# A two-layer trunk on one core: stored head outputs turned among the last projections, the last head's second half behind half 0, adds inside an MLP product, and four residual tiles in other buffers

## The chip, the cores and the metric

The kernel runs on one core of a Trainium2 chip. The metric is the device time of one execution in microseconds (us), as the median of the timed runs. The engines are TensorE (PE; its weight loads are PEld), VectorE (DVE), ScalarE (ACT), GpSimd (POOL) and SyncE (SP), whose queue issues nearly all the transfers (DMA). Each engine works through its own instructions in order; semaphores join them.

## The reference, cut to what matters

One sequence of 1024 tokens with 1024 features passes two layers in fp32. Layer 0 mixes with a gated MLP and a gated delta rule, layer 1 with differential attention over 8 heads. Each layer then has a squared-ReLU MLP and a gated per-layer embedding.

```python
def reference(x, p, ...):
    h = x
    for layer in range(DEPTH):                      # DEPTH = 2
        if layer % 2 == 0:
            ...
            h = h + jnp.concatenate([a_out, b_out], axis=-1) @ w_out_e[i]
        else:
            hn = rms_norm(h, ln_mix_o[i])
            o = diff_attention(hn @ w_qkv_o[i], attn_q_gain[i], attn_k_gain[i], diff_lambda[i],
                               attn_sub_gain[i], lam_init)
            h = h + o @ w_out_o[i]
        hn = rms_norm(h, ln_mlp[layer])
        h = h + jnp.square(jax.nn.relu(hn @ w_mlp1[layer])) @ w_mlp2[layer]
        gate = jax.nn.sigmoid(rms_norm(h, ln_ple[layer]) @ w_ple_gate[layer])
        h = h + (p[layer] @ w_ple_proj[layer]) * gate
    return h
```

## The kernel before, in words

**Layout.** Activations lie with features on the partitions: 8 tiles of 128 features (index m), each split into two halves of 512 tokens (index h, "half 0" and "half 1"). Every fp32 operand is split into a rounded part `hi` and a remainder `lo` (ScalarE casts, VectorE subtracts), and `mm3` makes three matmuls of each product. Large products use Strassen-like schemes: seven products of half-size operands with sums before and after them.

**Order.** A scheduler that simulates the engines decides the order of instructions within the data dependences and pool buffers; the order in which the code is written only breaks ties. `pe.floor` and `behind` add an order without a wait. Generators interleave streams that are independent.

**Stages in time.** Layer 0's mixing runs to about 490 us, its MLP to about 1130, its embedding to 1210; attention from 1210 to about 1720; `mix_out` (the output projection) to 1764; the second MLP to 2400; `ple_out`, the last stage, to the end.

**Attention (`attention`).** `pump` is called 264 times. Each call pulls units of the q, k and v projections as `MARKS` demands (168 units in all; a mark (i, u) says that u units are done by call i), and after call `TAIL` also steps `tails`. Of each head's output, `o` is scaled on GpSimd (line 1099) and stored in `o_dram`. `put_halves` loads the stored outputs of heads 0 to 5 through a ring of four tiles (`ol`), and `put_o` turns each with four transposes into a `tr` tile of PSUM, from which `ohi` (ScalarE) and `olo` (VectorE) are made. `mix_part` multiplies these heads with their part of the output weights and writes the sum to `h_dram`. Head 7 is the last; its outputs are turned directly by two closures in `close`. `ss` (line 938) and `qk` are tiles of a head's score path.

**`mix_out(h, ...)`.** It adds the remaining heads (`KA` = (6, 5): from head 6 in half 0, from head 5 in half 1) for each m: it loads `a` from `h_dram`, multiplies, adds (line 1257), squares into the sum `sqs` (lines 240, 241) and stores. After half 0, `rms(0, ...)` sums `sqs` over partitions with `ones` (tile `aux`), takes the mean `ms` (256), the power on GpSimd (258), broadcasts the row factors into `rb` with four matmuls and a copy (265), and scales the eight tiles into `hi` and `lo` (1268, 1272, 1273) for the MLP. In half 1 the same follows at the start of the MLP. For layer 0 `late` lets the first two output tiles begin with the operands that are there first.

**MLP.** `product2(n)` is one of the seven products of the second matrix (in the order 1, 6, 5, 3, 7, 4, 2). Its loop over 16 kt makes the left operand (`left`, adds on line 282), loads and splits the right one (`g`), and multiplies. `u` holds sums shared between the products, which are added into `acc`.

**`ple_out`.** Also seven products. Weight halves come through a ring of eight raw tiles (`raw`, line 653) and are combined by VectorE (643). `by_token` holds the activations written back token by token (522), from which residual rows are read (703). The norm of half 1 (`ones`, `ms`) is taken in the middle of the first product.

Of the kernel before, what the change touches and what calls it, by code (L numbers as in the profile page):

```python
# [18 lines left out]
P = 128  # L19
# [13 lines left out]
MARKS = ((64, 50), (192, 144), (223, 168))  # L33
TAIL = 220
# [80 lines left out]
class Trunk:  # L115
# [132 lines left out]
    def rms(self, half, sqs, ms=None, rows=True):  # L248
# [10 lines left out]
        rb = None  # L259
        if rows:  # L260
            pb = self.aux_ps()
            for t in range(4):
                self.pe.matmul(pb[:, t * P : (t + 1) * P], lhsT=r[:, t : t + 1].to_broadcast([P, P]), rhs=self.ident, start=True, stop=True)
            rb = self.sp.tile([P, HT], F32, tag=f"rb{half}", name=self.nm("rb"), bufs=1)
            nc.scalar.copy(rb, pb)
        return r, rb

    def mlp(self, x, x_tags, gain, w1, w2, gain_next, h_dram, p, last):
# [358 lines left out]
    def ple_out(self, pT, acc, by_token, gain, wg, wpj, out):  # L634
# [115 lines left out]
        rows(0, 0, [self.raw(1, HT)[:, 0] for _ in R])  # L750
# [142 lines left out]
    def attention(self, w_qkv, w_out, gain_next, h_dram):  # L893
# [219 lines left out]
        def put_halves():  # L1113
# [42 lines left out]
        def tails():  # L1156
            puts = put_halves()
            for hf in range(2):
# [70 lines left out]
    def mix_out(self, h, acc, w_out, h_dram, gain_next, k0=0, late=0):  # L1229
# [6 lines left out]
        for m in range(KT):  # L1236
# [6 lines left out]
            if late and m == 0:  # L1243
                begun.append(self.mm_ps())
                for q, k in itertools.product(range(2), range(late, n)):
                    self.mm3((ps, begun[0])[q], w.at(k, slice(q * P, (q + 1) * P)), self.mixed[h][k0 + k], k == late, False)
                    yield
            for i in range(n - late if late and m < 2 else 0, n):
                k = (i + late) % n
# [4 lines left out]
                self.pe.floor = None  # L1254
                if i < n - 1:
                    yield
# [5 lines left out]
        if h == 0:  # L1262
            self.rb[0] = self.rms(0, self.sqs[0])[1]
            self.rb_mark = self.pe.mark
            lows = []
            for m in range(KT):
                a = acc(m)
                inst = nc.vector.scalar_tensor_tensor(a, a, gain_next[:, m : m + 1], self.rb[0], ALU.mult, ALU.mult)
                if m > 1:
                    self.pe.behind(inst, lows[m - 2])  # L1270
                hi, lo = self.hs_new[0][m] = self.hs_parts(0, m)
                nc.scalar.copy(hi, a)  # L1272
                lows.append(nc.vector.tensor_tensor(lo, a, f32(hi), ALU.subtract).ins.name)  # L1273
# [7 lines left out]
    def even_mix(self, first, rows_of_rest, rest_of_x, w_in, ws, bs, conv, a_log, dt_bias, v_gain, o_gain, masks, w_out, gain_next, h_dram):  # L1281
# [539 lines left out]
        def mixing():  # L1821
# [10 lines left out]
            yield from beside(self.mix_out(0, acc, w_out, h_dram, gain_next, late=G), side, 4, 8)  # L1832
# [110 lines left out]
def trunk(tc, x, p, ln_mix_e, w_in_e, gmlp_v_gain, gmlp_ws, gmlp_bs, gdn_conv, gdn_a_log, gdn_dt_bias, gdn_out_gain,  # L1943
          w_out_e, ln_mix_o, w_qkv_o, attn_q_gain, attn_k_gain, diff_lambda, attn_sub_gain, w_out_o, ln_mlp, w_mlp1,
          w_mlp2, ln_ple, w_ple_gate, w_ple_proj, masks, out):
    with ExitStack() as ctx:
# [54 lines left out]
        for layer in range(2):  # L2001
# [15 lines left out]
            for _ in T.mix_out(1, lambda m: acc_of(m, 1), (w_out_e, w_out_o)[layer][0], h_dram, gain[3 * layer + 1], KA[1] * layer):  # L2017
# [52 lines left out]
```

## Time and profile before

| quantity | value |
|---|---|
| median of 3 runs | 2499.21 us (2496.64 to 2500.72) |
| profiled execution | 2507.63 us, its span 2505.9 us |
| mean granted TensorE clock | 0.997 |
| PE busy | 2472.7 us, 99% of the span, 13567 matmuls |
| DVE, ACT, POOL busy | 1866.3, 1289.0, 301.9 us |
| chain that ended last | PE 89%, DMA 4%, DVE 4% |
| DMA read, written | 322.95 MB, 136.33 MB |

A row of waits names the engine, the tile that it works on, the engine and tile that it waited for with the line in the kernel, and then the total, the number of times and the longest. A row of a timeline gives the start, the duration, the engine, the line, the operation, out<-in with the shape, and in brackets the idle time before it with its releaser. Busy times of PE include the pipelined end of a matmul.

### The profile page before, as it was taken

The numbers are of one execution on the slowest core, as the hardware profiler recorded it, in microseconds if no ns is written. First come the engines' busy times: TensorE is split into PE (matmuls) and PEld (weight loads), VectorE is DVE, ScalarE is ACT, GpSimd is POOL, SyncE is SP. The second block draws the span as 40 slices with busy tenths as digits, with TensorE's granted clock in tenths as the row PEclk, the third lists the DMA queues.
The fourth block names the chain that finished last, engine by engine and source line by source line (L and its number), as shares of the span: only waits on it lengthen the run. The fifth ranks groups of instructions, "written<-read, shape, count | busy, mean of one in ns | idle before, by whom it ended". The sixth has DMA issues, their size and how long they took to land.

```text
span 2505.9 us, 39836 instructions
## 1 busy us (share of the span) xinstructions
PE 2472.7 (99%) x13567; PEld 2109.4 (84%) x13567; DVE 1866.3 (74%) x3643; ACT 1289.0 (51%) x2584; POOL 301.9 (12%) x272
## 2 busy tenths in 40 slices
PE   9999999999999999999999999999999999999999
PEld 7898897888888877888899999987788888888877
DVE  7777876688667879566568888885886677788678
ACT  6543443465455434454456766664654455445443
POOL 0211230000000000000234443431000000000000
PEclk9999999999999999999999999999999999999999
DMA  8384645457556856553347776799375558657873
GB/s 251 115 246 110 169 144 172 142 163 237 175 190 214 264 173 201 183 175 118 115 99 168 162 170 157 168 244 285 127 231 194 178 186 282 214 186 204 234 218 110
DMA packets 567924, 461.96 MB, mean 184 GB/s; under 512 B 256676, under 2 KB 429736, under 8 KB 567720
## 3 DMA queue, kind: packets, MB, share of 16 engines
q1 hardware_dynamic: 533912, 455.21, 60.3%
q10 hardware_dynamic: 33808, 4.20, 1.1%
q8 instruction: 107, 1.75, 0.3%
q14 instruction: 97, 0.79, 0.1%
HBM read 322.95 MB, written 136.33 MB: 183 GB/s over the span
## 4 chain that ended last, share of the span: by engine, by line
PE 89%; DMA 4%; DVE 4%; issue 1%; SPq 1%; ACT 1%; POOL 0%; ACTq 0%; DVEq 0%; POOLq 0%
PE mm L76 78%; PE po L76 3%; PE qk L76 3%; PE aux L76 2%; DMA raw<-in_w_ple_gate_dram 1%; PE tr L79 1%; DMA raw<-in_w_mlp_dram 0%; DVE w L222 0%; DMA spill<-early 0%; DMA guv<-uv_dram 0%; PE pvn L76 0%; PE aux L79 0%; PE pkq L76 0%; PE pks L76 0%; PE py L76 0%
## 5 line engine op out<-in xcount | busy, mean ns | idle before, releaser
L76 PE MATMUL mm<-g,w 128*128 128x512 f32 x2592 | 603.6, 395 | 2.3 <-DVE acc L282 1.8
L221 ACT CAST w<-raw 128x512 fp32r<-128x512 f32 x598 | 364.9, 616 | 445.7 <-PE mm L76 355.5
L76 PEld LDWEIGHTS mm<-g,w 128*128 128x128 f32 x2592 | 486.8, 188 | 116.7 <-ACT g L221 2.2
L76 PE MATMUL mm<-hi,w 128*128 128x512 f32 x1728 | 554.9, 397 | 0.3 <-ACT hi L1272 0.3
L76 PE MATMUL mm<-w,hi 128*128 128x256 f32 (+2 forms) x2528 | 505.7, 295 | 3.0 <-ACT t L1499 2.5
L222 DVE TENSOR_TENSOR w<-raw,w 128x512 fp32r<-128x512 f32 (+1 forms) x510 | 349.0, 691 | 172.8 <-ACT w L221 162.5
L76 PEld LDWEIGHTS mm<-w,hi 128*128 128x128 f32 x2528 | 403.4, 189 | 18.2 <-ACT t L1499 2.7
L76 PEld LDWEIGHTS mm<-hi,w 128*128 128x128 f32 x1728 | 324.9, 189 | 73.8 <-ACT hi L1272 0.7
L76 PE MATMUL mm<-w,lo 128*128 128x256 f32 (+2 forms) x1264 | 369.1, 293 | 0.8 <-DVE lo L222 0.8
L76 PE MATMUL mm<-lo,w 128*128 128x512 f32 x864 | 341.3, 395 | 0.9 <-DVE lo L1273 0.9
L76 PE MATMUL mm<-t,w 128*128 128x512 f32 x1152 | 270.7, 394 | 1.2 <-ACT w L221 1.2
L76 PEld LDWEIGHTS mm<-t,w 128*128 128x128 f32 x1152 | 216.6, 188 | 52.1 <-ACT w L221 1.6
L76 PEld LDWEIGHTS mm<-w,lo 128*128 128x128 f32 x1264 | 238.8, 189 | 6.8 <-DVE lo L222 1.2
L76 PEld LDWEIGHTS mm<-lo,w 128*128 128x128 f32 x864 | 163.2, 189 | 37.8 <-DVE lo L1273 1.4
L222 DVE TENSOR_TENSOR g<-graw,g 128x512 fp32r<-128x512 f32 x216 | 147.5, 687 | 10.4 <-DMA gd<-g 7.2
L221 ACT CAST g<-graw 128x512 fp32r<-128x512 f32 x216 | 132.7, 617 | 40.3 <-DMA graw<-gd 15.1
L1048 ACT ACTIVATE lg<-lg,nm 128x128 f32<-128x128 f32 (+7 forms) x128 | 99.2, 776 | 79.0 <-DVE nm L1045 78.1
L258 POOL TENSOR_TENSOR r<-ms,mhalf 128x4 f32<-128x4 f32 x12 | 12.9, 1072 | 1003.6 <-DVE ms L256 978.0
L222 POOL TENSOR_TENSOR w<-raw,w 128x512 fp32r<-128x512 f32 (+1 forms) x88 | 115.5, 1332 | 142.6 <-ACT w L221 93.5
L348 ACT ACTIVATE g<-g 128x512 f32<-128x512 f32 x96 | 60.5, 631 | 117.9 <-DVE g L282 114.1
L1045 DVE CUSTOM_DVE_ANT_0 lg<-qk,al 128x512 f32<-128x512 f32 (+3 forms) x128 | 74.7, 587 | 25.8 <-PE qk L76 19.9
L76 PE MATMUL mm<-ohi,w 128*128 128x512 f32 x256 | 86.8, 405 | 0.5 <-DVE t L1225 0.5
(331 smaller groups left out, 3523.0 us busy)
## 6 DMA issues: line engine op xcount, KB each, us to landing
raw<-in_w_mlp_dram SPq DMA_DIRECT2D x352, 256.0 KB, 3.5
graw<-gd SPq DMA_DIRECT2D x224, 256.0 KB, 3.0
gd<-g SPq DMA_DIRECT2D x192, 256.0 KB, 3.1
raw<-in_w_ple_gate_dram SPq DMA_DIRECT2D x76, 256.0 KB, 3.6
acc<-h_dram SPq DMA_DIRECT2D x64, 256.0 KB, 4.4
keep<-in_w_mlp_dram SPq DMA_DIRECT2D x64, 256.0 KB, 4.5
raw<-in_w_in_e_dram SPq DMA_DIRECT2D x60, 256.0 KB, 3.8
h_dram<-acc SPq DMA_DIRECT2D x48, 256.0 KB, 2.7
```

The costliest lines, as they stand in the source:

```text
L76: self._next(self.engine.matmul(*a, **k))
L79: self._next(self.engine.transpose(*a, **k))
L221: self.nc.scalar.copy(hi, src)
L222: (lo_engine or self.nc.vector).tensor_tensor(lo, src, f32(hi), ALU.subtract)
L258: nc.gpsimd.tensor_tensor(r, ms, self.mhalf[:, 0:4], ALU.pow)
L348: nc.scalar.activation(g, src, AF.Relu)
L1045: nc.vector.tensor_tensor_reduce(out=lg[:, k0:k1], in0=ps[:, : k1 - k0], in1=al[:, u0 + k0 : u0 + k1], scale=-1.0, scalar=3.0e38 if c == 0 ...
L1048: nc.scalar.activation(lg[:, :n], lg[:, :n], AF.Exp, bias=nm[:, r, nch - 1 : nch], scale=-1.0, accum_out=me.sums[:, b, r : r + 1])
```

## The change

1. `MARKS` and `TAIL` are other numbers, and `put_halves` pauses after its first four loads. So those loads and the six turns of half 0 start as soon as 160 units are done, among the last projections, which now reach up to call 227.
2. In `mix_out` of layer 1, head 7's second half is turned after all of half 0 rather than in its middle, and the first two tiles of half 1 begin with heads 5 and 6. The sum of squares of half 0 stays behind half 0; the broadcast of the row factors and the scaling are deferred (`self.later`) to tile m = 4 of half 1.
3. In the fifth product of both layers' MLP, eight adds of `u` get places at kt 6 to 13; four stay behind the product.
4. In `ple_out`, the four residual rows (0, 0, q) are loaded into tiles of another pool (`lo1q`), no longer into the raw ring.

```diff
-MARKS = ((64, 50), (192, 144), (223, 168))
-TAIL = 220
+MARKS = ((64, 50), (192, 144), (227, 168))
+TAIL = 205
...
-        rb = None
-        if rows:
-            pb = self.aux_ps()
...
-        return r, rb
+        return r, self.rows(half, r) if rows else None
+
+    def rows(self, half, r):
+        pb = self.aux_ps()
...
-        def product2(n, ps=None, beside={}):
+        def product2(n, ps=None, beside={}, adds={}):
...
+                if kt in adds:
+                    q, m, h = adds[kt]
+                    tt(acc[m][h], acc[m][h], u[q], ALU.add)
...
-        ps = product2(5, beside={4: (0, 4), 8: (0, 0), 12: (1, 4)})
+        ps = product2(5, beside={4: (0, 4), 8: (0, 0), 12: (1, 4)}, adds={**{6 + q: (q, 4 + q, 0) for q in range(4)}, **{10 + q: (q, q, 0) for q in range(4)}})
...
-            for m, h in ((q, 0), (4 + q, 0), (4 + q, 1)):
-                tt(acc[m][h], acc[m][h], u[q], ALU.add)
+            tt(acc[4 + q][1], acc[4 + q][1], u[q], ALU.add)
...
-        rows(0, 0, [self.raw(1, HT)[:, 0] for _ in R])
+        rows(0, 0, [self.hp.tile([P, HT], F32, tag=f"lo1{q}", name=self.nm("rows")) for q in R])
...
             for n in range(4):
                 load(n)
+            yield
...
             puts = put_halves()
+            next(puts)
...
-                if h == 1 and k0 and (m, i) == (6, 0):
-
-                    self.pe.floor = self.rb_mark
+                if h == 1 and k0 and (m, i) == (4, 0):
+                    self.pe.floor = self.pe.mark
+                    self.later()
+                    self.pe.floor = None
...
-            self.rb[0] = self.rms(0, self.sqs[0])[1]
-            self.rb_mark = self.pe.mark
+            self.r[0] = self.rms(0, self.sqs[0], rows=False)[0]
+
+            def rows():
+                self.rb[0] = self.rows(0, self.r[0])
...
+            self.later = rows
+            if not k0:
+                self.later()
...
-                    if n + 1 in (4 * (KT - KA[0]), 6 * (KT - KA[0])):
+                    if n + 1 in (4 * (KT - KA[0]), 8 * (KT - KA[0])):
                         close.pop(0)()
-            for _ in T.mix_out(1, ..., KA[1] * layer):
+            for _ in T.mix_out(1, ..., KA[1] * layer, first=(0, 1) if layer else ()):
```

Three places in the order. The first is PE at the start of the last head: `tr<-ol` is a turn of a stored output, `mm<-ohi,w` the output projection, `po<-v,aT` a value product. Before:

```order
L79 MATMUL tr_18080<-ident,ol_18021 128x128 x2
L76 MATMUL po_18091<-v_16712,aT_17934 128x128 x4
L76 MATMUL po_18091<-v_16712,aT_17936 128x128
L76 MATMUL mm_18197<-ohi_18031,w_18179 128x512
L76 MATMUL mm_18197<-olo_18032,w_18179 128x512
L76 MATMUL mm_18197<-ohi_18031,w_18180 128x512
L76 MATMUL mm_18197<-ohi_18066,w_18179 128x512
L79 MATMUL tr_18100<-ident,ol_18021 128x128 x4
```

Now, where `mm<-w,lo` and `mm<-w,hi` of 256 columns are projections:

```order
L76 MATMUL mm_18051<-w_17394,lo_12434 128x256
L76 MATMUL mm_18051<-w_17394,hi_12437 128x256
L79 MATMUL tr_17952<-ident,ol_17676 128x128 x4
L76 MATMUL mm_18051<-w_17395,hi_12437 128x256
L76 MATMUL qk_18035<-ks_17269,qh_17822 128x512
L76 MATMUL qk_18035<-ks_17269,ql_12490 128x512
```

The turns of half 0 moved from among the output projection to among the projections of the last heads.

The second is PE in `mix_out`, around the turn of head 7's second half (`tr<-ident,o`). Before, the products behind it (`mm_19224`) are still of half 0:

```order
L76 MATMUL mm_19372<-olo_19078,w_19313 128x512
L76 MATMUL mm_19372<-ohi_19077,w_19314 128x512
L79 MATMUL tr_19214<-ident,o_18776 128x128 x4
L76 MATMUL mm_19224<-ohi_19068,w_19177 128x512
L76 MATMUL mm_19224<-olo_19069,w_19177 128x512
L76 MATMUL mm_19224<-ohi_19068,w_19178 128x512
```

Now half 0 ends twelve rows above this piece, and `mm_19325` and `mm_19278` are of half 1:

```order
L76 MATMUL mm_19325<-olo_19078,w_19266 128x512
L76 MATMUL mm_19325<-ohi_19077,w_19267 128x512
L76 MATMUL aux_19249<-ones,sqs_19112 128x1 x4
L79 MATMUL tr_19240<-ident,o_18785 128x128 x4
L76 MATMUL mm_19278<-ohi_18781,w_19260 128x512
L76 MATMUL mm_19278<-olo_18782,w_19260 128x512
```

The turn moved behind half 0 and its sum of squares, which stands directly in front of it.

The third is DVE in `ple_out`, from the last square of half 1 (`sqs`) to the mean `ms`; `raw<-raw,raw` is a difference of two weight halves, `w<-raw,w` a remainder. Before:

```order
L241 TENSOR_TENSOR sqs_24915<-sqs_24915,t_25400 128x512
L222 TENSOR_TENSOR w_25594<-raw_25590,w_25593 128x512
L222 TENSOR_TENSOR w_25601<-raw_25597,w_25600 128x512
L643 TENSOR_TENSOR raw_25828<-raw_25828,raw_25830 128x512
L222 TENSOR_TENSOR w_25834<-raw_25828,w_25833 128x512
L643 TENSOR_TENSOR raw_25837<-raw_25837,raw_25839 128x512
L256 TENSOR_SCALAR ms_25533<-aux_25528 128x4
```

Now:

```order
L241 TENSOR_TENSOR sqs_24915<-sqs_24915,t_25400 128x512
L222 TENSOR_TENSOR w_25594<-raw_25590,w_25593 128x512
L639 TENSOR_TENSOR raw_25837<-raw_25837,raw_25839 128x512
L222 TENSOR_TENSOR w_25601<-raw_25597,w_25600 128x512
L222 TENSOR_TENSOR w_25834<-raw_25828,w_25833 128x512
L639 TENSOR_TENSOR raw_25846<-raw_25846,raw_25848 128x512
L222 TENSOR_TENSOR w_25843<-raw_25837,w_25842 128x512
L639 TENSOR_TENSOR raw_25855<-raw_25855,raw_25857 128x512
L256 TENSOR_SCALAR ms_25533<-aux_25528 128x4
```

The first difference moved in front of the last square, and two further ones in front of `ms`. On SP the weight loads moved up to where the row loads stood, and the row loads into the MLP's seventh product.

More of the change, by code (lines that the diff above doesn't have):

```diff
@@ L258, in rms @@
         nc.gpsimd.tensor_tensor(r, ms, self.mhalf[:, 0:4], ALU.pow)
-        rb = None
-        if rows:
-            pb = self.aux_ps()
[L262 to L265, printed above, removed]
-        return r, rb
+        return r, self.rows(half, r) if rows else None
+    def rows(self, half, r):
+        pb = self.aux_ps()
+        for t in range(4):
+            self.pe.matmul(pb[:, t * P : (t + 1) * P], lhsT=r[:, t : t + 1].to_broadcast([P, P]), rhs=self.ident, start=True, stop=True)
+        rb = self.sp.tile([P, HT], F32, tag=f"rb{half}", name=self.nm("rb"), bufs=1)
+        self.nc.scalar.copy(rb, pb)
+        return rb
     def mlp(self, x, x_tags, gain, w1, w2, gain_next, h_dram, p, last):
@@ L1226, in mix_part, with mix_out @@
             nc.sync.dma_start(h_dram[m, :, cols], res)
-    def mix_out(self, h, acc, w_out, h_dram, gain_next, k0=0, late=0):
+    def mix_out(self, h, acc, w_out, h_dram, gain_next, k0=0, first=()):
         nc = self.nc
@@ L1831, in mixing @@
             side = second_gates()
-            yield from beside(self.mix_out(0, acc, w_out, h_dram, gain_next, late=G), side, 4, 8)
+            yield from beside(self.mix_out(0, acc, w_out, h_dram, gain_next, first=range(G, KT)), side, 4, 8)
             for _ in side:
```

32 lines of the change are left out of this document (16 added, 16 removed).

## The prediction

> **What bounds the kernel now.** I read the page's busy lines first.
>
> ```profile
> span 2505.9 us, 39836 instructions
> PE 2472.7 (99%) x13567; PEld 2109.4 (84%) x13567; DVE 1866.3 (74%) x3643; ACT 1289.0 (51%) x2584; POOL 301.9 (12%) x272
> ```
>
> TensorE works for 2472.7 of 2505.9 us, so 33.2 us are idle in all. The change takes no matmul away. Hence the whole stake is a part of those 33.2 us, plus time lost at a lower clock. Next came the PE's waits over the whole span, then those of 1600 to 1820 us, of 2400 to 2450 and of 930 to 955. The columns are the total, the times and the longest.
>
> ```profile
> PE aux L76 <- DVE ms L256: 2.5, 1, 2.5
> PE tr L79 <- POOL o L1099: 2.1, 1, 2.1
> PE po L76 <- DMA aT<-a_dram: 2.0, 3, 0.9
> PE mm L76 <- DVE acc L282: 1.8, 1, 1.8
> PE tr L79 <- DVE ss L938: 1.6, 1, 1.6
> ...
> PE mm L76 <- ACT w L221: 1.2, 1, 1.2
> PE tr L79 <- PE qk L76: 1.0, 1, 1.0
> PE mm L76 <- DVE lo L1273: 0.9, 1, 0.9
> PE mm L76 <- DVE t L1225: 0.5, 2, 0.3
> PE tr L79 <- DMA ol<-o_dram: 0.5, 1, 0.5
> PE mm L76 <- ACT hi L1272: 0.3, 1, 0.3
> ...
> PE mm L76 <- DVE lo L222: 0.8, 1, 0.8
> PE mm L76 <- ACT hi L221: 0.4, 1, 0.4
> ...
> PE mm L76 <- DVE g L222: 0.5, 1, 0.5
> ```
>
> These rows add up to 16.1 us, and all of them stand in the four places that the change touches. (The 1.8 and the 0.5 on `g` are at 937 and 950 us; the 2.5, the 0.8 and the 0.4 in the output stage; all else lies between 1613 and 1815.) Most is one late operand at a time. To see what a wait costs beside its own length, I asked for the granted clock around the 2.1 us wait and around the 2.5 us one. Each row is one 3.41 us stretch: length, busy time of PE, PEld, DVE, ACT and POOL, clock, DMA share, GB/s.
>
> ```profile
> 1741.27:1744.68 3.41, 1.38 (x6) 0.76 (x5) 0.81 (x3) 0.00 (x0) 2.25 (x3) 1.00 1.06 393
> 1744.68:1748.09 3.41, 3.38 (x10) 2.90 (x11) 1.44 (x2) 1.40 (x3) 0.00 (x0) 0.50 0.16 62
> ...
> 2417.14:2420.56 3.42, 1.80 (x8) 1.13 (x6) 0.71 (x2) 1.68 (x3) 0.00 (x0) 1.00 0.86 250
> 2420.56:2423.97 3.41, 2.49 (x11) 2.08 (x12) 2.81 (x7) 1.34 (x3) 1.01 (x1) 1.00 0.47 144
> ```
>
> In the first stretch PE idled 3.41 − 1.38 = 2.03 us, and the next ran at half clock: it lost half of 3.41, 1.7 us. The longer wait fell across two stretches (1.62 and 0.92 idle) and cost no clock. So one stretch with about 2 us idle is enough here, and a wait can be longer without penalty if it straddles. The Trainium skill's "TensorE: Matmul & The Clock Gate", section "Why this matters for your kernels", warns only of idle gaps above about 3 us; the row above, with a 2.06 us gap, disagrees, and the measurement decides. By that rule no wait forecast below could halve the clock, and the sum would be 0.4 us better.
>
> One matmul of 512 columns costs 50/216 = 0.23 us, one DVE operation of 128x512 follows the last at 0.60 us:
>
> ```profile
> 2200.00:2250.00 50.00, 50.00 (x216) 40.28 (x215) 46.82 (x77) 20.35 (x36) 0.00 (x0) 1.00 0.60 189
> ...
> 1737.47 0.68 DVE L1257 TENSOR_TENSOR acc<-acc,mm 128x512 f32<-128x512 f32 x1
> 1738.07 0.69 DVE L222 TENSOR_TENSOR w<-raw,w 128x512 fp32r<-128x512 f32 x1
> ```
>
> **Part 1, adds in the fifth product: −0.5.** The 24 adds `acc<-acc,u` (12 a layer) stay as many. In layer 0 eight of twelve already ran inside product 5; only the four on the last group come behind it, and only these move. DVE is then 4 × 0.60 = 2.4 us lighter after the product. That does not reach the 1.8 us wait, whose add stands behind operand work that itself waited for a load:
>
> ```profile
> 932.72 0.69 DVE L282 TENSOR_TENSOR raw<-raw,keep 128x512 f32<-128x512 f32 x1 [1.81 <-DMA raw<-in_w_mlp_dram]
> ...
> 941.73 1.90 DVE L282 TENSOR_TENSOR acc<-acc,u 128x512 f32<-128x512 f32 x3
> ```
>
> The three late adds at 941.73 end 6.3 us before the 0.5 us wait at 950, whose `g` is behind them on DVE; that wait goes. Inside the product the extra adds are hidden by PE's operands being ready early. Without that cover they would cost 2.4. Bounds: −1 to +1, since eight of their kind already ran there without a wait. Layer 1 shows no wait at this place: 0.
>
> **Part 2, transposes amid the projections: −2.8.** The six turns of the first half (24 transposes) used to begin when no projection was left, and then filled the start of the last attention head. There the 1.6 and the 1.0 us waits stood. Now they run among projection matmuls, and 17, 7 and 11 matmuls stand between the last head's own first turns. Both waits go: −2.6. Its first score product has about 3.0 us of other work in front of it, where it had 3.5: I charge +0.5. The second half of the last value product, which waited 0.7 for its probabilities, is now behind 48 matmuls of the output projection (11 us): −0.7.
>
> ```profile
> 1720.75 0.49 PE L76 MATMUL po<-v,aT 128*128 128x128 f32 x2 [0.74 <-DMA aT<-a_dram]
> 1700.00:1750.00 50.00, 46.22 (x211) 37.01 (x210) 24.81 (x41) 17.00 (x33) 7.47 (x8) 0.97 0.91 293
> 1650.00:1700.00 50.00, 49.12 (x269) 41.82 (x268) 39.18 (x95) 30.81 (x77) 17.85 (x17) 1.00 0.90 245
> ```
>
> The rest of the `aT` row, the `ol` and the `t` rows are transfers. DMA is busy for 0.90 of this time, and the change takes no byte away: they stay, possibly elsewhere. The four early ring loads wait for nobody, but they pass loads on SP. Bounds: −3.8 to 0.
>
> **Part 3, last head behind a half, norm rows later: −2.7.** Before, the last head's second turn was in the middle of half 0:
>
> ```profile
> 1741.95 0.16 DVE L1095 TENSOR_SCALAR osq<-osq 128x4 f32<-128x4 f32 x1
> ...
> 1742.25 1.01 POOL L1097 TENSOR_TENSOR of<-osq,mhalf 128x4 f32<-128x4 f32 x1 [30.41 <-DVE osq L1095]
> 1743.34 0.20 POOL L1098 TENSOR_TENSOR of<-of,c 128x4 f32<-128x4 f32 x1
> 1743.62 1.04 POOL L1099 TENSOR_TENSOR o<-o,of 128x512 f32<-128x512 f32 x1
> ```
>
> DVE finishes `osq` at 1742.1, GpSimd needs until 1744.66, PE stands 2.1 us and then loses 1.7 at half clock. Behind the half, four things go: 2.1 + 1.7, and, because 36 matmuls (8.3 us) instead of 9 (2.1 us) now stand between the broadcast of the row factors and their first use, the 0.3 and the 0.9 of `hi` and `lo`. That is −5.0.
>
> Two new waits come. (a) The sum of squares (`aux<-ones,sqs`) now has only 12 matmuls, 2.8 us, behind the last product of half 0. DVE has one add, two weight splits, three squares and `osq` to do: 6 × 0.60 + 0.2, and its last 0.1: 3.9. PE stands about 1.2. (b) The turn comes right behind. `osq` is now done one square earlier, about 1.3 us before that; GpSimd takes 1744.66 − 1742.1 = 2.6. PE had 0.5 of sums to do: 2.6 − 1.3 − 0.5, about +0.7. Together +1.9, in two pieces. They would have to lie in one stretch of the clock to reach 2: one chance in four of 1.7, so +0.4. Queued behind (b) on PE is the whole of half 1; on DVE, behind the sums, only the mean for the row factors.
>
> The 1.2 us wait on `w` at 1814 stands behind later operands of the same chain; I leave it. Half 1's own norm comes 35 rows (8 us) later in PE's order while its cover falls from 92 to 68 matmuls (21 to 16 us). I follow DVE through it at 0.60 each: some 3 us remain to spare, so nothing. If that cover is gone, see the first rival. Bounds: −6.2 (neither new wait) to 0 (both twice as long, a half-clock stretch and 1.4 more at the norm).
>
> **Part 4, residual rows off the ring: −1.8.** In the output stage four of the eight buffers were held by residual rows, so DVE waited for weight halves, in order, with `ms` behind them:
>
> ```profile
> DVE raw L643 <- DMA raw<-in_w_ple_gate_dram: 9.2, 7, 2.2
> ...
> 2416.47 0.69 DVE L643 TENSOR_TENSOR raw<-raw,raw 128x512 f32<-128x512 f32 x1 [2.22 <-DMA raw<-in_w_ple_gate_dram]
> 2420.66 0.69 DVE L643 TENSOR_TENSOR raw<-raw,raw 128x512 f32<-128x512 f32 x1 [2.12 <-DMA raw<-in_w_ple_gate_dram]
> 2421.27 0.15 DVE L256 TENSOR_SCALAR ms<-aux 128x4 f32<-128x4 f32 x1
> ...
> 2413.82 2.13 SPq L522 DMA_DIRECT2D by_token<-t  x4
> ...
> raw<-in_w_ple_gate_dram SPq DMA_DIRECT2D x25, 256.0 KB, 3.8
> ```
>
> With all eight free the first loads go out where the row loads stood. But the order now also puts *more* in front of `ms`: the subtractions of the third and fourth weight pair as well. The last of these loads follows four `by_token` stores on SP (2.13 us), so it goes out near 2416 and lands 3.8 later; subtraction and `ms` end near 2420.4. PE reached the waiting product at 2421.4 − 2.5 = 2418.9; three more matmuls now stand before the sum, so it gets there near 2419.6. So 2.5 shrinks to about 0.9: −1.6. The chain to `hi` and `lo` is no longer behind such loads: −0.4 and −0.3 of 0.8. The fourth projected product now waits for a DVE step that stands behind two more subtractions: +0.5. The four row loads move some 125 us forward, into the seventh product of the MLP, where their slots are free. They are 1 MB, 4 us of DMA at the 250 GB/s above, ahead of operand loads on SP whose users have work queued: nothing, and +1 at worst, a quarter of that. Bounds: −3.7 to +1.
>
> **The sum.** −0.5 − 2.8 − 2.7 − 1.8 = −7.8. The profiled execution took 2507.63 us (span 2505.9 and 1.7 around it), so 2499.8; it is 8.4 above the median of the three timed runs, 2499.21. The saving is made of waits that every execution has, so the median should be 2499.2 − 7.8 = 2491.4. A measurement of this kernel can tell about 0.2%, 5 us, from no change.
>
> **Rivals.**
>
> *DVE becomes the bound at the start of the MLP: slower.* In 1750 to 1850 DVE is busy 88 of 100 us:
>
> ```profile
> 1750.00:1850.00 100.00, 97.57 (x435) 78.73 (x434) 88.12 (x145) 62.24 (x113) 2.39 (x2) 1.00 0.49 159
> ```
>
> That is 12 us free. If the interleaved norm rows of both halves hold DVE for their casts (0.6 each, 16 rows: 10 us), PE has to wait for the last operands of each row. With the 3 us spare that is 7 us late; half 1's adds and squares held likewise cost 5 more, and two stretches at half clock 3.4. From −7.8 that is +7.6: 2507. It decides when PE's idle time between 1750 and 1850, now 2.4, exceeds about 14. For it: DVE is in order and nearly full. Against: the norm rows of half 0 begin well before their first use. Chance 0.11.
>
> *The transfers only move the waits: same.* DMA is at 0.90 from 1650 to 1750. If the attention turns now wait for their loads in place of the scores (2.6 back), the new pair (a), (b) costs twice what I gave (1.9 more) and `ms` remains as late (1.6), −1.7 is left: 2497.5. For it: the same queue. Against: the two long waits named are not on DMA. Chance 0.19.
>
> *All covers hold: faster still.* No wait at (a) or (b), `ms` in time, all first-use waits gone: the best bounds, −1 − 3.8 − 6.2 − 3.7 = −14.7, 2484.5. Chance 0.10.
>
> *The change does not do what it says.* For the adds this is nearly so: eight of twelve were early already. It is in the sum.
>
> **The numbers.** The forecast has 0.60 of the chance, with a range of its own from 2487 to 2496; about a tenth of it (0.05) lies above 2494.2, the bound of faster. Faster: 0.55 + 0.10 = 0.65, and 0.03 from the better end of the second rival: 0.68. Same: 0.05 + 0.16 = 0.21. Slower: 0.11. The range runs from the sum of the best bounds, 2484.5, to that of the worst, +1 + 0 + 0 + 1 on 2499.2, 2501: it leaves out the slow rival and little else.
>
> **What would show it.** Right: no wait on `o` inside half 0, no half-clock stretch near 1740, two short waits at the sum of squares and the turn behind it; no wait on `ss`; an `ms` wait under 1.5 us and DVE's weight waits in the output stage well under 9.2. Wrong: a half-clock stretch after the new pair, `ms` as late as before, PE idle over 5 us from 1750 to 1850, or waits of similar length on `aT` and `ol`.

## The result, and the profile after

The changed kernel took 2504.14 us (median of 12, 2499.17 to 2509.01) against 2500.16 us before (12 executions on the same chip): ratio 1.0018, 95% interval 1.0010 to 1.0026. It is 4 us slower, where 7.8 us less were forecast, and 3.1 us above the top of the range. Its profiled execution took 2503.71 us.

The busy lines of its page say that TensorE did the same work and stood idle 31.1 us instead of 33.2:

```profile
span 2502.0 us, 39857 instructions
PE 2470.9 (99%) x13567; PEld 2109.2 (84%) x13567; DVE 1866.4 (75%) x3643; ACT 1289.2 (52%) x2584; POOL 304.1 (12%) x272
```

PE's waits over the whole span, in the columns of the rows before (total, times, longest):

```profile
PE mm L76 <- DVE t L1223: 4.1, 2, 2.8
PE mm L76 <- DVE acc L276: 3.2, 2, 1.8
...
PE mm L76 <- DVE t L222: 2.0, 1, 2.0
...
PE aux L76 <- DVE sqs L241: 1.7, 1, 1.7
PE qk L76 <- DVE ql L1007: 1.6, 1, 1.6
...
PE aux L76 <- DVE ms L256: 1.3, 1, 1.3
...
PE aux L76 <- DVE t L714: 0.6, 1, 0.6
PE tr L79 <- POOL o L1095: 0.4, 1, 0.4
...
PE tr L79 <- DVE ks L995: 0.3, 1, 0.3
```

The waits on `ss`, `qk`, `hi` and `lo` are gone, as forecast. Those on `aT` and `ol`, most of which the forecast had left standing, are gone as well. Others took their place. From 1600 to 1850 us, the attention's end and the start of the MLP, the rows before add up to 2.1 + 2.0 + 1.6 + 1.2 + 1.0 + 0.9 + 0.5 + 0.5 + 0.3 = 10.1 us, and these to 4.1 + 2.0 + 1.7 + 1.6 + 0.4 + 0.3 = 10.1. Not a tenth was saved there. (PE's 1.8 on `acc` at 934 and the output stage's 1.3 and 0.6 are outside; so is a new 1.45 on `acc` at 2215.)

What the same sum costs has changed. These rows are windows of one clock stretch each: length, busy time of PE, PEld, DVE, ACT and POOL, granted clock, DMA share, GB/s.

```profile
1635.05:1638.47 3.42, 0.93 (x6) 0.53 (x4) 2.41 (x5) 1.88 (x4) 1.26 (x2) 1.00 0.87 255
1638.47:1641.88 3.41, 3.02 (x7) 2.44 (x8) 3.01 (x10) 2.41 (x7) 0.39 (x1) 0.50 1.06 351
1740.87:1744.28 3.41, 1.31 (x10) 0.97 (x8) 1.97 (x5) 0.00 (x0) 2.69 (x4) 1.00 1.06 396
1744.28:1747.69 3.41, 3.37 (x10) 2.88 (x11) 0.75 (x1) 0.69 (x1) 0.95 (x1) 0.50 0.22 76
1819.37:1822.79 3.42, 1.40 (x6) 1.18 (x7) 3.42 (x7) 0.39 (x1) 0.00 (x0) 1.00 0.51 141
1822.79:1826.20 3.41, 3.41 (x10) 2.61 (x9) 3.41 (x7) 2.18 (x4) 0.00 (x0) 0.50 0.08 23
```

Three times PE idled 2.0 to 2.5 us of a stretch and the next ran at half clock: at the last head's start, at the sums of half 0, and at the MLP's third product. Before there was one such place in this region, at 1745. The last head's start before, in the same view, had both its waits (1.56 and 0.98), in different stretches, and kept its clock:

```profile
1632.04:1635.46 3.42, 2.15 (x15) 1.63 (x14) 3.33 (x8) 2.60 (x8) 3.28 (x3) 1.00 0.87 211
1635.46:1638.87 3.41, 3.12 (x19) 2.49 (x20) 3.28 (x10) 2.53 (x5) 1.64 (x1) 1.00 1.05 357
1638.87:1642.28 3.41, 3.35 (x17) 2.65 (x16) 3.35 (x4) 2.58 (x6) 1.29 (x1) 1.00 0.72 261
1642.28:1645.70 3.42, 2.50 (x23) 2.53 (x24) 2.42 (x8) 2.76 (x10) 1.27 (x1) 1.00 0.70 191
```

Over all executions the mean granted clock was 0.9953 after, and 0.9971 to 0.9976 before (three other groups of 33 or 34 executions; the clock of the 12 executions of before beside the changed kernel is not on record). What it takes if PE always has work, (1 − clock) × 2500, is 11.7 us after and 6.0 to 7.3 before. The difference, 4.4 to 5.7, is an estimate; it is as large as the whole loss of 4.0.

VectorE's timeline after shows where the new waits come from (start, duration, line, and in brackets the idle time before it):

```profile
1634.72 0.69 DVE L933 TENSOR_REDUCE ss<-t 128x8 f32<-128x512 f32 x1
1635.33 1.24 DVE L1057 STREAM_TRANSPOSE lg<-lg 128x1024 f32<-128x1024 f32 x1
1636.60 0.48 DVE L1007 SCALAR_TENSOR_TENSOR ql<-tr,qg,qh 64x256 fp32r<-64x256 f32 x1
1637.00 0.15 DVE L934 SCALAR_TENSOR_TENSOR ss<-ss,e 128x8 f32<-128x8 f32 x1
1638.12 0.69 DVE L1223 TENSOR_TENSOR t<-t,mm 128x512 f32<-128x512 f32 x1 [0.97 <-DMA t<-h_dram]
...
1701.01 1.34 DVE L1223 TENSOR_TENSOR t<-t,mm 128x512 f32<-128x512 f32 x2 [2.47 <-DMA t<-h_dram]
```

The last projection's sum of squares (`ss`) now runs inside the last head's start. It and a transpose stand ahead of the head's `ql`, for which the first score product waits 1.6. The output projection of the stored heads now comes earlier as well. Its add of `t` waits for the residual that is loaded from `h_dram`: 0.97 and 2.47 us on VectorE, 1.24 and 2.85 on PE behind it.

### The profile page after: what moved, and what is told of

Its sections match the earlier page's. It is cut to its first block, busy times and chain, and to the rows that moved or that the text cites. A ratio compares the mean times of both kernels' runs of the same rounds, so it can differ in the third digit from the quotient of the medians.

```text
span 2502.0 us, 39857 instructions
## 1 busy us (share of the span) xinstructions
PE 2470.9 (99%) x13567; PEld 2109.2 (84%) x13567; DVE 1866.4 (75%) x3643; ACT 1289.2 (52%) x2584; POOL 304.1 (12%) x272
## 4 chain that ended last, share of the span: by engine, by line
PE 91%; DVE 3%; DMA 3%; issue 1%; ACT 0%; SPq 0%; POOL 0%; ACTq 0%; DVEq 0%; POOLq 0%
PE mm L76 80%; PE po L76 3%; PE qk L76 3%; PE aux L76 2%; DMA raw<-in_w_ple_gate_dram 1%; PE tr L79 1%; DMA t<-h_dram 1%; DVE w L222 1%; DMA guv<-uv_dram 0%; PE pvn L76 0%; DMA raw<-in_w_mlp_dram 0%; PE aux L79 0%; DMA diag<-early 0%; PE pkq L76 0%; PE pks L76 0%
## 5 line engine op out<-in xcount | busy, mean ns | idle before, releaser
L221 ACT CAST g<-graw 128x512 fp32r<-128x512 f32 x216 | 132.7, 617 | 31.9 <-PE mm L76 10.2
```

Of the source, the lines that this page charges most:

```text
L221: self.nc.scalar.copy(hi, src)
```

## The experiments

All kernels of a group ran on one chip with their own executions of the kernel before (medians 2499.4, 2500.1, 2499.9, 2503.8 and 2502.0 us for the five groups; one execution of 5517 us is left out). The first group is only1 to only4, the second marks_only to fill, the third after223, marks225, fill0 and best; the pauses make the last two. Ratios are to the executions of before in the same group. "Lost" is (1 − mean clock) × 2500 us.

| kernel | what it is | median us | ratio to before, 95% | mean clock, lost |
|---|---|---|---|---|
| before | the first three groups | 2499.4, 2500.1, 2499.9 | | 0.9976, 0.9971, 0.9972: 6.0, 7.3, 6.9 |
| after | all four parts | 2504.1 | 1.0018 (1.0010 to 1.0026) | 0.9953, 11.7 |
| only1 | adds in the fifth product | 2499.7 | 1.0006 (0.9997 to 1.0015) | 0.9971, 7.3 |
| only2 | turns early, projections later | 2504.4 | 1.0019 (1.0010 to 1.0027) | 0.9960, 10.0 |
| only3 | edits in `mix_out` | 2501.8 | 1.0006 (0.9997 to 1.0015) | 0.9967, 8.2 |
| only4 | residual rows off the ring | 2499.4 | 0.9998 (0.9989 to 1.0006) | 0.9975, 6.4 |
| marks_only | projections later alone | 2507.4 | 1.0023 (1.0012 to 1.0034) | 0.9960, 10.0 |
| turns_only | turns early alone | 2502.4 | 1.0007 (0.9996 to 1.0017) | 0.9968, 8.0 |
| without2 | after without part 2 | 2498.5 | 0.9995 (0.9984 to 1.0006) | 0.9969, 7.7 |
| fill | after, 27 useless matmuls | 2501.7 | 1.0000 (0.9990 to 1.0010) | 0.9973, 6.8 |
| after223 | after, projections as before | 2500.6 | 1.0000 (0.9992 to 1.0009) | 0.9964, 9.1 |
| marks225 | before, `MARKS` at 225 | 2502.8 | 1.0008 (0.9999 to 1.0017) | 0.9964, 9.1 |

**The parts alone.** Each of four kernels is the one before with one part of the change.

```diff
-        ps = product2(5, beside={4: (0, 4), 8: (0, 0), 12: (1, 4)})
+        ps = product2(5, beside={...}, adds={...})
...
-MARKS = ((64, 50), (192, 144), (223, 168))
-TAIL = 220
+MARKS = ((64, 50), (192, 144), (227, 168))
+TAIL = 205
...
-            for i in range(n - late if late and m < 2 else 0, n):
+            for i in range(len(first) if m < 2 else 0, n):
...
-        rows(0, 0, [self.raw(1, HT)[:, 0] for _ in R])
+        rows(0, 0, [self.hp.tile([P, HT], F32, tag=f"lo1{q}", name=self.nm("rows")) for q in R])
```

> The kernel before with the eight adds in the fifth product alone. Theory (each part's waits and clock stretches, summed from the two profiles, add up): +0.9 us, from a new 1.45 us wait on acc behind layer 1's fifth product less the 0.5 us wait on g in layer 0. Rival (the adds are free and the new wait comes from other parts' shifts): 0 or -0.5 us.

> The kernel before with MARKS, TAIL and the early ring loads alone. Theory (the loss sits here: DVE's adds of residual tiles t wait for loads from h_dram that now come late): +2.3 us or more, with waits mm <- DVE t of 1 to 3 us near 1640 and 1700. Rival (the loss sits in mix_out): -2 to 0 us, and no such waits.

> The kernel before with the mix_out edits alone (last head's second half behind half 0, norm rows deferred). Theory (sums from the profiles): +1.4 us, with waits of about 1.7 and 0.4 us at the sum of squares and the turn, one half-clock stretch there, and a wait on w about 60 us later. Rival (part 2 causes what is seen there): -3 to -2 us.

> The kernel before with the residual rows in other buffers alone. Theory: -1.8 us, the ms wait near 1.3 us and a new wait of 0.6 us on the projected product. Rival (the DMA of the rows holds back the MLP): 0 or more.

Only part 2 is measurably slower, by as much as the whole change. The other three can't be told from no change. The gain that I gave to part 3, 2.7 us or 0.11%, lies outside only3's interval; those of parts 1 and 4, 0.02% and 0.07%, are too small for these intervals to exclude. For part 4 the profiles say more. The wait on `ms`, 2.5 us in the profile before, varies from profile to profile, with the part and without it. PE's waits in the output stage of only4 (which has part 4), of only1 and of marks225 (which don't):

```profile
PE aux L76 <- DVE ms L256: 2.6, 1, 2.6
```

```profile
PE aux L76 <- DVE ms L256: 1.0, 1, 1.0
```

```profile
PE aux L76 <- DVE ms L256: 0.9, 1, 0.9
```

All waits of PE over 0.15 us from 2395 to 2450 add up to 1.4 to 3.7 us, 2.3 on average, in eight profiles without part 4 (before, at 3.7, is the highest), and to 1.9 to 2.6, on average 2.2, in six with it. So the part saves about 0.1 us by this measure, not 1.8.

**Part 2 taken apart and taken out.** marks_only moves only `MARKS`, turns_only only `TAIL` and the ring's first loads; without2 is the change with both undone.

```diff
-MARKS = ((64, 50), (192, 144), (223, 168))
+MARKS = ((64, 50), (192, 144), (227, 168))
```

```diff
-TAIL = 220
+TAIL = 205
...
             for n in range(4):
                 load(n)
+            yield
```

> The kernel before with MARKS alone (projections due by call 227 instead of 223; TAIL and the ring loads as before). Theory (the early turns make the last head start with little work behind it and its adds of t late): about half or less of part 2's +4.7 us, 0 to +1.5 us. Rival (the later projections alone push the tail's transfers together): +3 us or more.

> The kernel before with the early ring loads and TAIL 205, MARKS as before. Theory: most of part 2's loss, +3 to +5 us, and a mean clock near 0.996. Rival (MARKS is the cause): 0 to +1.5 us, clock as before, 0.9976.

> The changed kernel with MARKS, TAIL and the ring loads as before. Theory (part 2 holds the loss, by clock stretches): within 2 us of the kernel before, mean clock 0.997. Rival (parts 1 and 3 lose as much together): +3 us or more.

My theory here, that the early turns hold most of the loss, fell. The mark alone costs 0.23% and the turns 0.07%, within their uncertainty of nothing. Without part 2 nothing is lost. The waits of marks_only at the last head's start, and the clock around them:

```profile
PE qk L76 <- DVE ks L999: 1.8, 1, 1.8
...
PE tr L79 <- PE qk L76: 0.9, 1, 0.9
PE tr L79 <- DVE olo L1110: 0.8, 1, 0.8
```

```profile
1635.27:1638.68 3.41, 1.23 (x6) 0.47 (x4) 3.38 (x6) 1.29 (x3) 3.26 (x3) 1.00 0.87 281
1638.68:1642.10 3.42, 2.15 (x9) 1.92 (x10) 2.76 (x9) 2.55 (x7) 1.16 (x1) 0.50 0.95 259
1642.10:1645.51 3.41, 3.41 (x17) 3.31 (x17) 1.33 (x3) 1.20 (x5) 0.00 (x0) 0.50 1.04 177
```

The last head begins at call 224. With the mark at 223 the last projection's `ss` runs on VectorE at 1633.60, 6.3 us ahead of the head's first `ks`; at 227 it stands 1.9 us ahead of it (1636.25 and 1638.16 in marks_only). Three waits then come within 6 us and cost two stretches, 3.4 us, beside their own 3.5, where the kernel before had 2.5 and no half clock. Over all executions the clock takes 2.7 us more than in its group's kernel before (10.0 against 7.3), about half of this kernel's loss; that its longer waits are the rest is an inference. The early turns are not free of half clock: the profile of turns_only has it at 1637, behind a wait of 1.5 us on `ks`, and at 1698, behind one of 2.2 us on `aT`, but not near 1745.

**Useless work in the new waits.** If the clock is what is lost, matmuls without a use in those waits should win time. fill is the change with 9 of them before the last head's first score product and 18 meant for the time ahead of half 0's sums of squares (13 of these ran earlier, about 1700). That is 27, one less than the expectation says.

```diff
+                    if hd == 7 and b == 0 and r == 0:
+                        for _ in range(9):
+                            self.pe.matmul(ps[:, P:], lhsT=qh[:, r, qs], rhs=ks[:, r, P:HT], start=True, stop=True)
```

> The changed kernel with 28 extra matmuls that compute nothing used: 9 at the last head's first score, 13 mostly in front of the wait near 1700, 6 in front of the sum of squares of half 0. They take PE time only where it waits anyway. Theory (the loss is time at half clock, set off by idle time that these matmuls fill): mean clock back to 0.997 or above and 3 to 5 us faster than the changed kernel, near 2500. Rival (the loss is the waits themselves): clock unchanged or no matter, time as the changed kernel, 2504, or up to 3 us slower for the extra work.

The clock's share fell from 11.7 to 6.8 us and the ratio to before from 1.0018 to 1.0000, with 27 matmuls more to do. No half clock was left at 1638 or 1744 in its profile; the one at the MLP's third product, 1820, stayed. The rival does not explain this: PE's idle time in the two profiles fell by 4.3 us (31.1 to 26.8), while the useless matmuls held PE for about 5.7 (36 steps of 0.11 and nine of 0.19), so filling alone saved nothing.

**The mark put back, and halfway.**

```diff
-MARKS = ((64, 50), (192, 144), (227, 168))
+MARKS = ((64, 50), (192, 144), (223, 168))
```

```diff
-MARKS = ((64, 50), (192, 144), (223, 168))
+MARKS = ((64, 50), (192, 144), (225, 168))
```

> The changed kernel with one number put back: the last projection is due at call 223 again, not 227; all else of the change stays. Before 2500, the change 2504.1. Theory: with the projection's last calls out of the last head's start (call 224), the waits there come 5 us or more apart and no longer halve the clock at 1638; what is left is the early turns (+2) and the small gains of the other parts: 2499 to 2501.5, ratio 0.9995 to 1.0006, and TensorE's mean clock back at 0.997. Rival: the late projections only fill what the early turns leave empty, so that without them the turns cost more: 2503 to 2506.

> The kernel before with the last projection due at call 225: halfway between before (223: 2500) and the run with 227 alone (2506 to 2507). Theory, a step: the last head starts at call 224, and any projection that is still open there puts its vector steps ahead of the head's first keys and queries: most of the loss is there already, 2503 to 2507, with one or two stretches of half clock at 1636 to 1646. Rival, a slope: the loss grows with the calls that are left, 2501.5 to 2503.5, and no half clock there.

after223 came out as the theory says in time: one number takes back the 4 us. The mean clock came back only to 0.9964, and its profile has half clock at 1702, 1746 and 1825 and none at 1638. marks225 is inconclusive: its median, 2502.8, is in the slope's range, while its profile shows the half clock at 1634 that the slope excluded.

**Useless work elsewhere, and a faster version.** fill0 puts useless matmuls into two waits of layer 0; best is without2 with these and with more at the squares and at the MLP's third product.

```diff
             pp = aux([P, G, P], "sc", "pkq")
             for h in range(G):
+                if c == 0 and h == G // 2:
+                    self.useless(6, pp[:, h])
...
+            if c == 0:
+                self.useless(11, pv[:, 0], solved_mark[0])
```

> The kernel before with nothing changed but useless matmuls of 128 columns in the first layer, far from every edit of the change: 6 ahead of the second half of the first chunk's q.k product (wait 1.36 at 206, with 1.84 behind it), and 11 ahead of the first chunk's pvn (wait 2.5 at 383.5). Theory: a wait of 2 us within one clock stretch costs 1.7 more at half clock; filled, the stretches at 208 and at 382 (two) go, and nothing else: 2495 to 2497.5, ratio 0.998 to 0.999, lost clock time down by 3 to 5 us. Rival: the half clock comes with what runs there (the products of 32 columns, the state's chain) and not with the wait: the useless work only fills idle time, 2499.5 to 2501.5.

> Parts 1, 3 and 4 of the change without part 2, with useless matmuls in four waits: the two places in the first layer as in fill0, 7 ahead of the first half's sums of squares (wait 1.4, turn 0.4 behind it), 9 ahead of the MLP's third product (wait 2.1 at 1820). The same version without them ran 2498.5 to 2499.4. Theory: three to five stretches of half clock less at 1.7 us each: 2492 to 2495, ratio 0.997 to 0.998, faster than both kernels. Rival: the useless work delays what is next in line by as much as the clock saves: 2498 to 2500.

The theory missed both. fill0 ran at 2501.2 us (ratio 1.0007, 0.9998 to 1.0016) and best at 2503.7 (1.0016, 1.0008 to 1.0025), slower. fill0's time lies in the rival's range, but the run does not test the rival: its 11 matmuls ran at 220 us, not at the wait, and the order after them changed, so that the 2.5 us wait on `xt` was now one on `alo`, at 377 to 379:

```profile
PE mm L76 <- DVE alo L1586: 2.4, 1, 2.4
```

So both places still have half clock in its profile, one stretch each, at 203 and 381. The lost time fell by less than forecast, to 5.5 us from 6.9, if one execution is left out: it has a mean clock of 0.946, by which it would have lost 135 us, and took 2507.2. That execution shows that the clock's record, or the product by which I turn it into time, can be wrong; "lost" is an estimate everywhere.

In best the clock did come back: its profile has one stretch of half clock before the end, and the loss is 6.1 us instead of without2's 7.7. But its 33 useless matmuls, two steps of 0.11 us each, held PE for about 7 us, and one wait only moved: the turn now stands ahead of the filled sums and waits longer for `o`, in two stretches. That cost more than the 1.6 us of clock.

```profile
PE tr L79 <- POOL o L1106: 2.9, 1, 2.9
```

I have no version that is measurably faster than before; the nearest, without2 and only4, are within their uncertainty of it.

**Pauses of one making, near and far.** The products with the MLPs' second matrix have hardly a wait. Into each of the 14 I put three pauses: ScalarE copies an operand tile onto itself between two groups of matmuls that read it, so the values stay and PE waits 0.8 us.

```diff
                 for q in range(4):
+                    if q in PAUSES.get(kt, ()):
+                        nc.scalar.copy(b[0], f32(b[0]))
+                        self.pe.floor = self.pe.mark
                     self.mm3(ps[q], ...)
+                    self.pe.floor = self.pe.mark if kt in PAUSES else None
```

`PAUSES` is {4: (1,), 8: (1,), 12: (1,)} in far, {8: (1, 2, 3)} in near3, {8: (1, 2), 12: (1,)} in near2, {7: (1,), 8: (1,), 9: (1,)} in spread.

> The kernel before with 42 pauses put into the MLPs' second products: ScalarE copies one operand tile onto itself between two groups of matmuls that read it, so TensorE waits for about 1.0 us (a copy of 128x512 took 0.63 to 0.72 in the profile, and the two handovers). Three pauses to a product, four k-steps (11 us) apart. Theory and rival both: 42 pauses at about 1.0, 35 to 50 us slower, no half clock in the products.

> The same 42 pauses, the three of a product in one k-step with 0.7 us of matmuls between them: 3 us idle within some 4.4. Theory (idle time summed over one clock stretch of 3.41 us halves the next): one or two stretches of half clock for each of 14 products, 1.7 each: 24 to 48 us more than with the pauses far apart, and 14 to 28 stretches in the clock's record. Rival (a wait costs its length): the same time as far within 3 us.

> The same 42 pauses, two of a product next to each other (2 us idle within 2.7) and the third 11 us off. Theory: a sum of 2 us is at the edge, and the place of the free-running stretch decides: half clock in some 5 to 14 of the 14 pairs, 8 to 24 us more than far. Rival: the same as far within 3 us.

> The same 42 pauses, one in each of three k-steps in a row, so one in about 3.8 us: no stretch of 3.41 us can hold much over 1.1 us of idle time. Theory: no half clock, the same time as far within 3 us. Rival, a shorter distance between pauses costs in itself whatever the sum in a stretch: between far and near3.

Medians: 2564.5, 2516.8, 2540.6 and 2548.6 us. This does not decide: the scheduler filled the pauses that stood together with the next k-step's matmuls. Of 42 pauses 37, 13, 25 and 40 are waits of PE in the four profiles. So near_held and far_held hold all matmuls in the order written:

```diff
-                    self.pe.floor = self.pe.mark if kt in PAUSES else None
+                    self.pe.floor = self.pe.mark
```

> The 42 pauses of far, three to a product and four k-steps apart, with all matmuls of the second products held in the order written. In far 37 of them showed as waits of 0.7 to 1.1 us (34 us in all), and the kernel took 60 us more. Both theories: as far within 8 us, 2555 to 2572, and no more than three stretches of half clock in the products.

> The 42 pauses of near3, three in one k-step, held in the order written: three waits of 0.8 with two blocks of 0.7 us between them, 2.4 us idle within 3.9. Theory (idle time summed over one free-running stretch of 3.41 us halves the next): half clock after 7 to 14 of the 14 groups, 12 to 24 us more than waits of the same sum cost far apart, and as many stretches in the clock's record. Rival (a wait costs its length only): no more than three stretches in the products, and the cost per us of wait as in far_held.

Medians 2556.6 (far_held; ratio 1.0214, 1.0190 to 1.0238) and 2556.2 (near_held; 1.0218, 1.0193 to 1.0243). The times are equal, which by itself speaks for the rival, but the sums of idle time are not. The waits on the pauses in far_held and in near_held, and each profile's span and clock:

```profile
PE mm L77 <- ACT g L506: 34.9, 36, 2.5
```

```profile
core 0: 2559.8 us, clock 0.995
```

```profile
PE mm L77 <- ACT g L506: 30.9, 39, 1.3
```

```profile
core 0: 2553.4 us, clock 0.991
```

All waits of PE over 0.15 us add up to 67.7 us in far_held and 55.1 in near_held. In far_held some waits grew to 2.5. In front of that one the copy itself came late, because ScalarE's cast ahead of it waited for an add on VectorE:

```profile
2173.26 0.62 ACT L222 CAST w<-raw 128x512 fp32r<-128x512 f32 x1 [1.26 <-DVE raw L283]
2173.79 0.61 ACT L222 CAST g<-graw 128x512 fp32r<-128x512 f32 x1
2174.31 0.61 ACT L506 CAST g<-g 128x512 fp32r<-128x512 f32 x1
```

Time at half clock was 20.5 us and 44.4 us before the last stretch of each. If half of that is lost, the sums are 67.7 + 10.2 = 77.9 and 55.1 + 22.2 = 77.3: what near_held saved in waits it paid in clock. This sum is rough, since the two profiled executions themselves are 6.4 us apart. The mean clocks of the four executions of each, 0.9962 and 0.9900, say the same: 9.4 and 25.0 us lost at equal times. Ten of near_held's stretches are in the products, behind 5 of the 14 groups: fewer than the 7 to 14 I expected. The three that far_held has in the products stand behind single waits of 2.1, 2.5 and 1.9 us, none behind a lone pause of 0.8. Two groups of near_held, one with half clock and one without:

```profile
820.95:824.36 3.41, 1.94 (x6) 0.97 (x6) 0.81 (x2) 1.18 (x4) 0.00 (x0) 1.00 0.60 215
824.36:827.78 3.42, 2.79 (x12) 2.31 (x13) 1.29 (x2) 1.72 (x3) 0.00 (x0) 1.00 0.71 253
1012.10:1015.51 3.41, 1.84 (x8) 0.87 (x7) 1.29 (x2) 2.13 (x4) 0.00 (x0) 1.00 0.68 173
1015.51:1018.93 3.42, 2.66 (x6) 1.65 (x7) 0.00 (x0) 0.62 (x1) 0.00 (x0) 0.50 0.60 216
1018.93:1022.34 3.41, 3.41 (x10) 2.63 (x9) 1.90 (x3) 1.14 (x2) 0.00 (x0) 0.50 0.00 0
```

No pause here is over 0.9 us. In the first group one stretch holds 3.41 − 1.94 = 1.47 us of idle time and the clock stays; in the second it holds 1.57 and two stretches are halved. So short waits do add up within a stretch, and where the stretch begins decides. Over all 14 groups the two kinds meet at one place: the fullest stretches of those without half clock hold up to 1.58 us of idle time, those with it 1.57 to 1.65.

## Why the prediction was wrong, step by step

**The step that failed: part 2, −2.8.** "Both waits go: −2.6 … I charge +0.5." They went. In their place stand 0.33, 1.65 and 1.24 us within 5 us (the score product alone is 1.65, not 0.5), and 2.85 on `t` at 1702 where 0.7 on `aT` was to be saved. I counted the matmuls in front of each product as cover, and did not ask what the moved work puts on VectorE, which works in order: the last projection's `ss` ahead of `ql`, and adds whose residuals are not there yet. That the early turns are to blame was my second error, made after the result; the mark is.

**The price of a wait.** "One chance in four of 1.7, so +0.4" was the only charge for half clock in the sum. In 1600 to 1850 alone, after has three stretches (5.1 us) where before has one. This is where the loss comes from: over all executions 4.4 to 5.7 us more go to the clock, and fill, which takes two of the three stretches away, takes the loss away. The sentence by the Trainium skill's rule, that no wait forecast could halve the clock, fell with it.

**Part 3, −2.7.** The two new waits were sized well: 1.73 at the sums (1.2 forecast) and 0.41 at the turn (0.7); the waits on `hi` and `lo` went. But the two pieces stand 1.5 us apart, and the profiles of after, only3, without2 and after223 all have half clock behind them. Four of four is not one in four. In three both pieces lay in one stretch. Nor does a stretch have to "reach 2": in after223 it held 1.42 us, and in without2 the wait at the sums began in the stretch before:

```profile
1737.22:1740.63 3.41, 2.90 (x13) 2.03 (x11) 3.41 (x8) 1.57 (x3) 1.00 (x1) 1.00 1.03 379
1740.63:1744.04 3.41, 2.10 (x15) 1.93 (x16) 0.90 (x3) 0.35 (x1) 3.12 (x4) 1.00 0.89 325
1744.04:1747.46 3.42, 3.42 (x10) 2.64 (x9) 0.75 (x1) 0.33 (x1) 0.00 (x0) 0.50 0.04 13
```

There 3.41 − 2.10 = 1.31 us was enough. And "the 1.2 on `w` at 1814: I leave it" became 2.0 to 2.4 on `t`: VectorE is full there, and half 1's rows come later. That place has half clock in after, only3, after223 and fill, not in without2. So the half clock only moved from 1745 to 1744, and one was added at 1822. only3 measured 1.0006. The bounds of this part were added up wrongly, too. By its own terms (both waits twice as long, a half-clock stretch and 1.4) the upper one is −5.0 + 3.8 + 1.7 + 1.4 = +1.9, not 0, which puts the top of the range at 2503.1, still under the measured time; and without the two new waits the saving is 5.0, not 6.2.

**Part 4, −1.8.** In the two profiles the stage's waits do fall, and so does VectorE's wait for its weights, from 9.2:

```profile
DVE raw L639 <- DMA raw<-in_w_ple_gate_dram: 7.4, 6, 2.4
```

But only4 measured 0.9998, with an `ms` wait of 2.6, and over fourteen profiles the stage's waits hardly differ with the part and without (2.2 and 2.3 us). The sentence "waits that every execution has" failed: I took one draw of a wait behind a transfer for the wait itself. The whole profile was such a draw: its 2507.63 us are exceeded by one of 126 executions of the kernel before, and its waits over 0.15 us add up to 28.8 us, those of only1 and only4 to 24.6 and 23.8. The 0.6 on the fourth projected product was forecast as 0.5.

**Part 1, −0.5.** Too small to measure (only1: 1.0006). The 0.5 on `g` at 950 went as forecast. Layer 1, which I put at 0, has a wait of 1.45 on `acc` in after and 0.9 in only1, and none in without2, after223 and fill, which have the same adds: it varies from profile to profile.

**The rivals.** "The transfers only move the waits" (0.19, 2497.5) had the mechanism of the new waits on `t`, without the clock. VectorE as the bound from 1750 to 1850 did not come: PE was busy 97.95 of those 100 us.

**What was to show it.** No wait on `o` inside half 0, none on `ss`, two short waits at the sums, `ms` under 1.5, the weight waits at 7.4 instead of 9.2: all there. "No half-clock stretch near 1740" failed, and with it one of the signs of wrong was there, half clock behind the new pair; the waits behind transfers came on `t`, not on `aT` or `ol`.

## What to carry to other kernels

Price a wait of TensorE by the stretch in which it falls: add up all waits within about 3.4 us, and where the sum reaches 1.9 us charge another 1.7 for the stretch behind it, from 1.5 to 1.9 about a third of that (the counts are below). When work moves to fill one engine's gaps, follow what it puts on the in-order engine beside it, and ask which wait comes next within 5 us. A wait behind a transfer that one profile shows may be a draw; take a second profile before putting it into a sum.

## What the runs showed of the hardware

The clock can be halved by sums of idle time smaller than the 2 us that I had assumed: by 1.57 us in one stretch above, made of two pauses of 0.8, and by 1.31 in without2. I counted the stretches of all twenty profiles that ran at full clock, without the first 15 and the last 8 us of each:

| PE idle in the stretch, us | stretches | next at half clock |
|---|---|---|
| 1.9 or more | 62 | 62 |
| 1.5 to 1.9 | 54 | 18 |
| 1.3 to 1.5 | 30 | 4 |
| 1.0 to 1.3 | 51 | 1 |
| under 1.0 | 14263 | 0 |

So the edge is not sharp by this measure. A stretch of after kept its clock with 3.42 − 1.58 = 1.84 us idle:

```profile
1699.91:1703.33 3.42, 1.58 (x7) 1.32 (x8) 2.33 (x3) 0.00 (x0) 0.00 (x0) 1.00 1.09 387
1703.33:1706.74 3.41, 3.41 (x17) 2.74 (x16) 2.15 (x4) 0.00 (x0) 0.00 (x0) 1.00 0.81 158
```

Why this one did and the one at 1012 in near_held did not stays open. PE's busy times include modelled ends, so the true idle time may differ; in without2 the busy time at the sums is that of eight matmuls of a single column.

The stretches are not tied to the program. In only1 the 2.0 us wait on `o` straddled two (1.35 and 0.70 us idle) and no half clock followed; in before a wait of the same length fell into one (2.03) and the next was halved. The Trainium skill's "TensorE: Matmul & The Clock Gate", Part 1, "What's actually happening", calls the window free-running, 3413 ns long; the trace agrees (stretches of 3.41 us). The same page's "Why this matters for your kernels" warns of idle gaps above about 3 us; here two pauses of 0.8 us in one stretch were enough.
